# Cross-covariance attention: loads in 4 KB rows, softmax of eight heads at once, V transposed to two partition halves, stores in 2 KB rows

## The chip, the cores and the metric

The kernel runs on one core of one Trainium2 chip. The metric is the device time of one execution in microseconds (us). Before the change it was 144.62 us (median of 3 runs, 144.57 to 145.19). The profile's span, from first to last instruction, is shorter than the time: by 1.5 us in the profiled run of this kernel.

"Slow" is a run more than 1.5% above the fastest of the same kernel. Ratios are the mean time of one kernel's fast runs over the mean of the other kernel's fast runs of the same rounds on the same chip, with a 95% interval, so they are not quite the ratio of the medians quoted beside them. Where I turn a difference of two ratios into microseconds I multiply it by 144.7, the time of the kernel before, and say so.

## The reference

```python
# Q, K, V: (8, 12, 512, 64) float32, so 96 heads of 512 rows x 64
Q_norm = Q / (np.linalg.norm(Q, axis=-2, keepdims=True) + 1e-10)   # norm over the 512 rows
K_norm = K / (np.linalg.norm(K, axis=-2, keepdims=True) + 1e-10)
attn = np.einsum('bhnd,bhne->bhde', Q_norm, K_norm)                # 64 x 64 per head
attn = softmax(attn, axis=-1)
return np.einsum('bhnd,bhde->bhne', V, attn)
```

The logits are 64 x 64 per head, so the arithmetic is small and 50.33 MB have to move: 37.75 in and 12.58 out.

Both kernels get the squared norms and the raw logits from one product. With Q and K of a head side by side as `[Q | K]`, the gram matrix `[Q | K]^T [Q | K]` has the squared norms of Q and K on its diagonal and Q^T K off it.

## The kernel before

Four heads are a unit, and there are 24 units. Row `n` of a head lies on partition `n // 4`, so that one partition's share of one head is 4 rows x 64 floats, 1 KB.

```python
T, HU, PU = 4, 4, 2
Qf = Q.rearrange("b h (p t) d -> p (b h) t d", p=128)       # K, V, out alike: 1 KB runs

def casts(u):                                               # all on VectorE
    ... four casts of Q and K halves into qkb ...
    nc.vector.tensor_copy(w.rearrange("p t h d -> p h t d"), vf[u])
def grams(u):                                               # 16 matmuls of 128 rows per unit
    for h in range(HU):
        for t in range(T):
            x = qkb[u][:, h, t, :]
            nc.tensor.matmul(o, x, x, start=(t == 0), stop=(t == T - 1))
# norms (4 masked reductions), power -0.5 on GpSimd, scale_k, logits, exps,
# normalise: each per unit, in pieces of two heads            ... cut ...
def vtrans(u):                                              # 8 transposes, 2 copies per unit
def outs(u):                                                # 8 matmuls, 2 copies per unit
```

Of the kernel before, what the change touches and what calls it, by code (L numbers as in the profile page):

```python
# [8 lines left out]
F32 = mybir.dt.float32  # L9
BF16 = mybir.dt.bfloat16  # L10
AF = mybir.ActivationFunctionType
ALU = mybir.AluOpType

D = 64
T = 4
HU = 4
PU = HU // 2


@with_exitstack  # L20
def kernel(
# [6 lines left out]
):  # L28
    nc = tc.nc
    B, H, N, _ = Q.shape  # L30
    assert N == 128 * T and Q.shape[3] == D
    BH = B * H
    U = BH // HU


    Qf = Q.rearrange("b h (p t) d -> p (b h) t d", p=128)
    Kf = K.rearrange("b h (p t) d -> p (b h) t d", p=128)
    Vf = V.rearrange("b h (p t) d -> p (b h) t d", p=128)
    Of = out.rearrange("b h (p t) d -> p (b h) t d", p=128)

    ctx.enter_context(tc.manual_schedule())

    const = ctx.enter_context(tc.tile_pool(name="const", bufs=1))
    qp = ctx.enter_context(tc.tile_pool(name="qp", bufs=5))
    vp = ctx.enter_context(tc.tile_pool(name="vp", bufs=5))
    vbp = ctx.enter_context(tc.tile_pool(name="vbp", bufs=3))
    qkp = ctx.enter_context(tc.tile_pool(name="qkp", bufs=4))
    vtp = ctx.enter_context(tc.tile_pool(name="vtp", bufs=4))
    sop = ctx.enter_context(tc.tile_pool(name="sop", bufs=10))
    small = ctx.enter_context(tc.tile_pool(name="small", bufs=4))  # L50
    ps_g = ctx.enter_context(tc.tile_pool(name="ps_g", bufs=2, space=bass.MemoryType.PSUM))
    ps_v = ctx.enter_context(tc.tile_pool(name="ps_v", bufs=2, space=bass.MemoryType.PSUM))
    ps_l = ctx.enter_context(tc.tile_pool(name="ps_l", bufs=2, space=bass.MemoryType.PSUM))
    ps_o = ctx.enter_context(tc.tile_pool(name="ps_o", bufs=2, space=bass.MemoryType.PSUM))

    LOAD_AHEAD = 3
    CAST_AHEAD = 1
    STORE_LAG = 6

    qf, kf, vf, vb, qkb, gram, nsq, kqs, rq, lg, ex, ab, vt, so = ({} for _ in range(14))  # L60

    def load_qk(u):
        qf[u] = qp.tile([128, HU, T, D], F32, name="qf")
        kf[u] = qp.tile([128, HU, T, D], F32, name="kf")
        nc.sync.dma_start(out=qf[u], in_=Qf[:, u * HU:(u + 1) * HU])  # L65
        nc.sync.dma_start(out=kf[u], in_=Kf[:, u * HU:(u + 1) * HU])  # L66

    def load_v(u):
        vf[u] = vp.tile([128, HU, T, D], F32, name="vf")
        nc.sync.dma_start(out=vf[u], in_=Vf[:, u * HU:(u + 1) * HU])  # L70

    def store(u):
        nc.sync.dma_start(out=Of[:, u * HU:(u + 1) * HU], in_=so[u])

    def casts(u):

        t_ = qkb[u] = qkp.tile([128, HU, T, 2 * D], BF16, name="qkb")
        nc.vector.tensor_copy(t_[:, 0::2, :, 0:D], qf[u][:, 0::2])  # L78
        nc.vector.tensor_copy(t_[:, 1::2, :, D:2 * D], qf[u][:, 1::2])  # L79
        nc.vector.tensor_copy(t_[:, 0::2, :, D:2 * D], kf[u][:, 0::2])  # L80
        nc.vector.tensor_copy(t_[:, 1::2, :, 0:D], kf[u][:, 1::2])  # L81

        w = vb[u] = vbp.tile([128, T, HU, D], BF16, name="vb")
        nc.vector.tensor_copy(w.rearrange("p t h d -> p h t d"), vf[u])  # L84

    def grams(u):
        g = gram[u] = ps_g.tile([128, PU, 4, D], F32, name="gram")
        for h in range(HU):
            o = g[:, h // 2, 2 * (h % 2):2 * (h % 2) + 2, :]
            for t in range(T):  # L90
                x = qkb[u][:, h, t, :]
                nc.tensor.matmul(o, x, x, start=(t == 0), stop=(t == T - 1))  # L92

    def norms(u):

        n2 = nsq[u] = small.tile([128, 2, PU], F32, name="nsq")
        for p in range(PU):
            for c, (blk, m) in enumerate(((gram[u][:, p, 0::3, :], mask_q), (gram[u][:, p, 1:3, :], mask_k))):
                scr = small.tile([128, 2, D], F32, name="scr")
                nc.vector.tensor_tensor_reduce(  # L100
                    out=scr, in0=blk, in1=m, scale=1.0, scalar=1e-20,
                    op0=ALU.mult, op1=ALU.add, accum_out=n2[:, c, p:p + 1],
                )
        r = rq[u] = small.tile([128, 2, PU], F32, name="rq")
        nc.gpsimd.tensor_tensor(out=r, in0=n2, in1=mhalf, op=ALU.pow)  # L105

    def scale_k(u):

        kk = kqs[u] = small.tile([128, PU, 2, D], F32, name="kqs")
        for p in range(PU):  # L110
            nc.vector.scalar_tensor_tensor(  # L111
                out=kk[:, p], in0=gram[u][:, p, 0::3, :], scalar=rq[u][:, 1, p:p + 1], in1=off_diag,
                op0=ALU.mult, op1=ALU.mult,
            )

    def logits(u):
        l = lg[u] = ps_l.tile([128, PU, D], F32, name="lg")
        for p in range(PU):
            nc.tensor.matmul(l[:, p, :], kqs[u][:, p].rearrange("p a d -> p (a d)"), eye2)  # L119

    def exps(u):
        e = ex[u] = small.tile([128, PU, D], F32, name="ex")
        s = small.tile([128, PU], F32, name="esum")
        for p in range(PU):
            nc.scalar.activation(e[:, p, :], lg[u][:, p, :], AF.Exp, scale=rq[u][:, 0, p:p + 1], accum_out=s[:, p:p + 1])  # L125
        ex[u] = (e, s)

    def normalise(u):
        e, s = ex[u]
        ri = small.tile([128, PU], F32, name="rinv")  # L130
        nc.vector.reciprocal(ri, s)  # L131
        a = ab[u] = small.tile([128, PU, 2, D], BF16, name="ab")
        for p in range(PU):
            nc.vector.scalar_tensor_tensor(  # L134
                out=a[:, p], in0=e[:, p, None, :].to_broadcast([128, 2, D]), scalar=ri[:, p:p + 1], in1=on_diag,
                op0=ALU.mult, op1=ALU.mult,
            )

    def vtrans(u):
        for p in range(PU):  # L140
            ps = ps_v.tile([128, T, 128], BF16, name="vps")
            for t in range(T):
                nc.tensor.transpose(ps[:, t, :], vb[u][:, t, 2 * p:2 * p + 2, :].rearrange("p h d -> p (h d)"), identb)  # L143
            w = vtp.tile([128, T, 128], BF16, name=f"vt{p}")
            nc.scalar.copy(w, ps)  # L145
            vt[u, p] = w

    def outs(u):
        s = so[u] = sop.tile([128, HU, T, D], F32, name="so")
        for p in range(PU):  # L150
            po = ps_o.tile([128, T, 2, D], F32, name="po")
            for t in range(T):
                nc.tensor.matmul(po[:, t], vt[u, p][:, t, :], ab[u][:, p].rearrange("p a d -> p (a d)"))  # L153
            nc.scalar.copy(s[:, 2 * p:2 * p + 2].rearrange("p h t d -> p t h d"), po)  # L154


    for u in range(LOAD_AHEAD):
        load_qk(u)
        load_v(u)

    ident = const.tile([128, 128], F32, name="ident")
    make_identity(nc, ident)
    identb = const.tile([128, 128], BF16, name="identb")
    nc.gpsimd.tensor_copy(identb, ident)
    mask_q = ident.rearrange("p (a d) -> p a d", a=2)
    swap = const.tile([128, 2, D], F32, name="swap")
    nc.gpsimd.tensor_copy(swap[:, 0, :], ident[:, D:])
    nc.gpsimd.tensor_copy(swap[:, 1, :], ident[:, :D])
    mask_k = swap
    eye2 = const.tile([128, D], F32, name="eye2")  # L170
    nc.gpsimd.tensor_tensor(out=eye2, in0=ident[:, :D], in1=ident[:, D:], op=ALU.add)
    blocks = const.tile([128, 3, D], F32, name="blocks")
    nc.gpsimd.memset(blocks, 0.0)
    nc.gpsimd.memset(blocks[0:D, 1, :], 1.0)
    nc.gpsimd.memset(blocks[D:, 0, :], 1.0)
    nc.gpsimd.memset(blocks[D:, 2, :], 1.0)
    off_diag = blocks[:, 0:2, :]
    on_diag = blocks[:, 1:3, :]
    mhalf = const.tile([128, 2, PU], F32, name="mhalf")
    nc.gpsimd.memset(mhalf, -0.5)  # L180

    for u in range(CAST_AHEAD):
        casts(u)
    for s in range(U + 2):
        if s + LOAD_AHEAD < U:
            load_qk(s + LOAD_AHEAD)
            load_v(s + LOAD_AHEAD)
        if 0 <= s - STORE_LAG:
            store(s - STORE_LAG)
        if s < U:  # L190
            grams(s)
            norms(s)
        if 0 <= s - 1 < U:
            logits(s - 1)
            exps(s - 1)
        if s < U:
            vtrans(s)
        if s + CAST_AHEAD < U:
            casts(s + CAST_AHEAD)
        if 0 <= s - 1 < U:  # L200
            normalise(s - 1)
        if s < U:
            scale_k(s)
        if 0 <= s - 2 < U:
            outs(s - 2)
    for u in range(U + 2 - STORE_LAG, U):
        store(u)


# [28 lines left out]
```

## Time and profile before

| | before |
|---|---|
| time, median | 144.62 us |
| span | 143.1 us |
| DMA | full in all slices but the first and last, 50701 packets, nearly all of 1 KB, 353 GB/s |
| VectorE | 100.9 us busy (71%) |
| TensorE | 95.3 us busy (67%), 864 matmuls and 864 weight loads |
| ScalarE, GpSimd | 64.8 us (45%), 29.9 us (21%) |

Read the DMA row first: it is what never rests. The engines' busy shares say that none is full. The list of DMA queues: queue, kind, packets, MB, share of sixteen engines.

```profile
q8 instruction: 6, 0.10, 0.3%
```

By the kind that the page gives it, this queue brings instructions, not data.

### The profile page before, as it was taken

Reading aid. Unit: us, or ns where it says so; the run is one execution under the profiler, and the core shown is the slowest. Engines: PE = TensorE matmul, PEld = TensorE weight load, DVE = VectorE, ACT = ScalarE, POOL = GpSimd, SP = SyncE. Lnnn points to the kernel's source line nnn. Section 1 sums busy time; section 2 is a strip of 40 time slices with the busy share of each in tenths; the row PEclk is TensorE's granted clock in tenths of the full one; section 3 lists DMA queues with packets and bytes.
Section 4 is the critical chain, followed back from the end, with each engine's and each line's share of the span. In section 5 each row is a group of like instructions: output and inputs, shape, how many; then the busy total and the mean of one; then the engine's idle time right before and its main releaser. Section 6 shows DMA issues by size and latency. Waiting matters only on the chain.

```text
span 143.1 us, 2715 instructions
## 1 busy us (share of the span) xinstructions
PE 95.3 (67%) x864; PEld 83.7 (59%) x864; DVE 100.9 (71%) x432; ACT 64.8 (45%) x193; POOL 29.9 (21%) x39
## 2 busy tenths in 40 slices
PE   0245879775896797686559874776795694397820
PEld 0234669664795686575557763765694683397620
DVE  0435888989888987696786886883868868767410
ACT  3003406764377644715706536437074273371840
POOL 6003302332033330311302303302022032031100
PEclk9999999999559856857975589655559559855555
DMA  4999999999999999999999999999999999999993
GB/s 133 336 353 349 348 348 351 350 348 348 348 350 348 376 370 378 368 371 384 368 372 380 372 376 379 371 380 371 375 369 369 371 382 372 382 377 386 377 322 113
DMA packets 50701, 50.49 MB, mean 353 GB/s; under 512 B 1536, under 2 KB 50688, under 8 KB 50688
## 3 DMA queue, kind: packets, MB, share of 16 engines
q1 hardware_dynamic: 50688, 50.34, 104.5%
q8 instruction: 6, 0.10, 0.3%
q14 instruction: 7, 0.06, 0.1%
HBM read 37.75 MB, written 12.58 MB: 352 GB/s over the span
## 4 chain that ended last, share of the span: by engine, by line
DMA 65%; DVE 14%; SPq 12%; PE 2%; ACT 1%; issue 1%; ACTq 0%
DMA vf<-in_V_dram 59%; DMA qf<-in_Q_dram 6%; SPq L65 5%; DVE vb L84 4%; SPq L66 4%; DVE ab L134 4%; SPq L70 3%; DVE scr L100 3%; DVE kqs L111 2%; PE lg L119 2%; ACT ex L125 1%; DVE rinv L131 1%; PE po L153 0%; ACT so L154 0%; DVE qkb L78 0%
## 5 line engine op out<-in xcount | busy, mean ns | idle before, releaser
L92 PE MATMUL gram<-qkb 128*128 128x128 bf16 x384 | 39.6, 283 | 20.0 <-DVE qkb L80 19.4
L105 POOL TENSOR_TENSOR rq<-nsq,mhalf 128x4 f32<-128x4 f32 x24 | 27.6, 1151 | 102.0 <-DVE nsq L100 102.0
L92 PEld LDWEIGHTS <-qkb 128*128 128x128 bf16 x384 | 33.8, 130 | 25.3 <-DVE qkb L80 24.6
L125 ACT ACTIVATE ex<-lg,rq 128x64 f32<-128x64 f32 x48 | 14.7, 310 | 63.2 <-PE lg L119 63.2
L119 PE MATMUL lg<-eye,kqs 128*128 128x64 f32 x96 | 22.8, 381 | 19.4 <-DVE kqs L111 19.3
L119 PEld LDWEIGHTS lg<-eye,kqs 128*128 128x128 f32 x96 | 18.8, 271 | 24.9 <-DVE kqs L111 24.9
L145 ACT COPY vt<-vps 128x512 bf16<-128x512 bf16 x48 | 25.7, 593 | 8.7 <-PE vps L143 8.7
L84 DVE CAST vb<-vf 128x1024 bf16<-128x1024 f32 x24 | 16.7, 694 | 15.2 <-DMA vf<-in_V_dram 15.2
L154 ACT COPY so<-po 128x512 f32<-128x512 f32 x48 | 26.4, 618 | 0.3 <-PE po L153 0.3
L143 PE MATMUL vps<-identb,vb 128*128 128x128 bf16 x192 | 20.9, 274 | 1.9 <-DVE vb L84 1.9
L153 PE MATMUL po<-ab,vt 128*128 128x128 bf16 x192 | 20.9, 274 | 0.6 <-DVE ab L134 0.6
L143 PEld LDWEIGHTS <-vb 128*128 128x128 bf16 x192 | 19.3, 138 | 2.2 <-DVE vb L84 2.2
L80 DVE CAST qkb<-kf 128x512 bf16<-128x512 f32 x24 | 10.2, 424 | 11.6 <-DMA kf<-in_K_dram 11.6
L153 PEld LDWEIGHTS <-vt 128*128 128x128 bf16 x192 | 17.4, 129 | 0.9 <-DVE ab L134 0.9
L134 DVE SCALAR_TENSOR_TENSOR ab<-ex,rinv,blocks 128x128 bf16<-128x128 f32 x48 | 14.7, 349 | 0.9
L111 DVE SCALAR_TENSOR_TENSOR kqs<-gram,rq,blocks 128x128 f32<-128x128 f32 x48 | 14.5, 344 | 0.0
L78 DVE CAST qkb<-qf 128x512 bf16<-128x512 f32 x24 | 10.2, 425 | 5.1 <-DMA qf<-in_Q_dram 5.1
L100 DVE CUSTOM_DVE_ANT_0 scr<-gram,swap 128x128 f32<-128x128 f32 x48 | 13.7, 286 | 0.0
L100 DVE CUSTOM_DVE_ANT_0 scr<-gram,ident 128x128 f32<-128x128 f32 x48 | 13.6, 284 | 0.0
L79 DVE CAST qkb<-qf 128x512 bf16<-128x512 f32 x24 | 10.1, 420 | 0.0
L81 DVE CAST qkb<-kf 128x512 bf16<-128x512 f32 x24 | 10.1, 419 | 0.0
L125 ACT ACTIVATION_READ_ACCUMULATOR ex<-lg,rq 128x1 f32 x48 | 9.4, 196 | 0.0
(18 smaller groups left out, 15.8 us busy)
## 6 DMA issues: line engine op xcount, KB each, us to landing
qf<-in_Q_dram SPq DMA_DIRECT2D x24, 512.0 KB, 8.3
kf<-in_K_dram SPq DMA_DIRECT2D x24, 512.0 KB, 8.4
vf<-in_V_dram SPq DMA_DIRECT2D x24, 512.0 KB, 8.4
out_dram<-so SPq DMA_DIRECT2D x24, 512.0 KB, 7.9
```

The costliest lines, as they stand in the source:

```text
L84: nc.vector.tensor_copy(w.rearrange("p t h d -> p h t d"), vf[u])
L92: nc.tensor.matmul(o, x, x, start=(t == 0), stop=(t == T - 1))
L100: nc.vector.tensor_tensor_reduce(out=scr, in0=blk, in1=m, scale=1.0, scalar=1e-20, op0=ALU.mult, op1=ALU.add, accum_out=n2[:, c, p:p + 1],)
L105: nc.gpsimd.tensor_tensor(out=r, in0=n2, in1=mhalf, op=ALU.pow)
L111: nc.vector.scalar_tensor_tensor(out=kk[:, p], in0=gram[u][:, p, 0::3, :], scalar=rq[u][:, 1, p:p + 1], in1=off_diag, op0=ALU.mult, op1=AL ...
L119: nc.tensor.matmul(l[:, p, :], kqs[u][:, p].rearrange("p a d -> p (a d)"), eye2)
L125: nc.scalar.activation(e[:, p, :], lg[u][:, p, :], AF.Exp, scale=rq[u][:, 0, p:p + 1], accum_out=s[:, p:p + 1])
L134: nc.vector.scalar_tensor_tensor(out=a[:, p], in0=e[:, p, None, :].to_broadcast([128, 2, D]), scalar=ri[:, p:p + 1], in1=on_diag, op0=ALU. ...
L143: nc.tensor.transpose(ps[:, t, :], vb[u][:, t, 2 * p:2 * p + 2, :].rearrange("p h d -> p (h d)"), identb)
L145: nc.scalar.copy(w, ps)
L153: nc.tensor.matmul(po[:, t], vt[u, p][:, t, :], ab[u][:, p].rearrange("p a d -> p (a d)"))
L154: nc.scalar.copy(s[:, 2 * p:2 * p + 2].rearrange("p h t d -> p t h d"), po)
```

## The change

The intent is fewer and longer DMA rows. Partition `32 h + p` now holds sixteen consecutive rows of head `h`: 16 x 64 floats, 4 KB, and a load of four heads is one contiguous block of 512 KB. The price is that a head has only 32 partitions, so its gram product needs 16 matmuls of 32 rows instead of 4 of 128. VectorE is relieved by doing norms, scaling, softmax and products for two units (eight heads, the two partition halves) at once, and by giving the V cast to GpSimd.

```diff
-T = 4
+T = 16
-    Qf = Q.rearrange("b h (p t) d -> p (b h) t d", p=128)
+    Qu = Q.rearrange("b h (p t) d -> (b h p) (t d)", t=T)           # 4 KB rows
+    Of = ... .rearrange("(s r i p x) -> s i p r x", r=2, i=2, p=128, x=J * D)   # 2 KB rows
     def grams(u):
-        g = ps_g.tile([128, PU, 4, D], F32)                # 2 buffers
+        g = ps_g.tile([128, HU, 512], F32)                 # 512 floats per head, 1 buffer
-        for h in range(HU):
-            for t in range(T):
-                x = qkb[u][:, h, t, :]
+        for t in range(T):
+            for h in range(HU):
+                x = qkb[u][32 * h:32 * (h + 1), t, :]
+                nc.tensor.matmul(g[:, h, 0:2 * D], x, x, ...)
+    def cast_v(u):
+        nc.gpsimd.tensor_scalar(out=vb[u], in0=v32[u], scalar1=1.0, scalar2=0.0, ...)
+    def squares(u):   # per unit: two diagonal picks, one copy of the K^T Q block, into halves
+    def norms(s):     # per pair: one reduction, one power (GpSimd)
+    def scale_k(s):   # per pair: kqs = kq * r
     def vtrans(s, k):
+        for c in range(2):
+            for j in range(J // 2):
+                for r in range(2):      # unit r of the pair to partition half r
+                    nc.tensor.transpose(ps[r * D:(r + 1) * D, c, j, :], vb[2 * s + r][:, t, :], identb)
     ... logits, exps, normalise, outs per pair of units; one buffer each of ps_g, ps_v, ps_l ...
+    for s in range(U + 4):              # the order in which each engine gets its work
+        p, odd = divmod(s, 2)
+        ... loads and stores ...
+        cast_qk(s + 1)
+        cast_v(s - 1)
+        if not odd: scale_k(p - 1)
+        if odd:     normalise(p - 1)
+        grams(s); squares(s)
+        if odd:     norms(p)
+        if not odd: outs(p - 2, 3); logits(p - 1); exps(p - 1); vtrans(p - 1, 0)
+        if odd:     vtrans(p - 1, 1); outs(p - 1, 0); outs(p - 1, 1); outs(p - 1, 2)
```

(Bounds tests on the last lines left out.)

## The prediction

Its sum came to 130.3 us of span along the last V and 128.3 for the transfers, so to 131.0 us of time. Three quarters of the bytes at 414 and one quarter at 393, its estimates from the packet records, give 408.5. Its "row groups" are the four sets of 32 partitions, one for each head of a unit. That matmuls on them run at once, and that GpSimd and VectorE can block each other, were assumptions: the trace of before shows neither.

> **What bounds the kernel now.** I read the slices of the page first, because they show whether one limit holds from end to end or whether stages differ.
>
> ```profile
> PE   0245879775896797686559874776795694397820
> DVE  0435888989888987696786886883868868767410
> ACT  3003406764377644715706536437074273371840
> PEclk9999999999559856857975589655559559855555
> DMA  4999999999999999999999999999999999999993
> GB/s 133 336 353 349 348 348 351 350 348 348 348 350 348 376 370 378 368 371 384 368 372 380 372 376 379 371 380 371 375 369 369 371 382 372 382 377 386 377 322 113
> DMA packets 50701, 50.49 MB, mean 353 GB/s; under 512 B 1536, under 2 KB 50688, under 8 KB 50688
> ```
>
> The DMA row is 9 in all slices but the first and the last, and no engine's row is. The GB/s row is flat, and it has two levels: about 349 while only loads run (slices 2 to 12), about 375 once stores are mixed in. The packet line says in what sizes: 50688 packets under 2 KB, of which 1536 are the small ones that signal a landing. The other 49152 carry 50.33 MB, so each is 1024 bytes. That is one (head, partition) row: 4 x 64 floats.
>
> Next the queue and the chain, to see whether the transfers themselves are what is waited for.
>
> ```profile
> q1 hardware_dynamic: 50688, 50.34, 104.5%
> ...
> DMA 65%; DVE 14%; SPq 12%; PE 2%; ACT 1%; issue 1%; ACTq 0%
> DMA vf<-in_V_dram 59%; DMA qf<-in_Q_dram 6%; SPq L65 5%; DVE vb L84 4%; SPq L66 4%; DVE ab L134 4%; SPq L70 3%; DVE scr L100 3%; DVE kqs L111 2%; PE lg L119 2%; ACT ex L125 1%; DVE rinv L131 1%; PE po L153 0%; ACT so L154 0%; DVE qkb L78 0%
> ```
>
> The packets' time fills all sixteen engines for the whole span and a bit more (packets overlap). The chain runs through the landing of loads for 65% of the span, and another 12% is the queue's own issuing. VectorE's 14% of the chain is work between a landing and a buffer coming free, not work that starves the DMA. The waits confirm the direction: VectorE waits for data, and TensorE waits for VectorE.
>
> ```profile
> PE gram L92 <- DVE qkb L80: 19.4, 16, 6.3
> ...
> DVE vb L84 <- DMA vf<-in_V_dram: 15.2, 24, 2.8
> DVE qkb L80 <- DMA kf<-in_K_dram: 11.6, 17, 1.4
> ```
>
> Last, a view by stretches, for the end.
>
> ```profile
> 20.00:36.00 16.00, 12.28 (x132) 10.94 (x133) 14.74 (x68) 9.60 (x31) 5.03 (x4) 0.99 1.10 349
> ...
> 84.00:108.00 24.00, 16.74 (x144) 14.79 (x144) 17.27 (x74) 10.56 (x32) 4.34 (x4) 0.64 1.09 374
> ...
> 130.00:143.00 13.00, 5.83 (x40) 5.03 (x40) 3.63 (x19) 5.38 (x16) 1.01 (x1) 0.50 0.84 292
> ```
>
> The columns are busy time of PE, weight loads, DVE, ACT and POOL, then the granted clock, the DMA share and GB/s. Full sharing is about 1.09; only the last 13 us fall short (0.84). So the kernel is bound by the rate at which 1 KB packets move, plus some 3 us lost at the end.
>
> [...]
>
> **The change part by part.**
>
> *Loads.* The same 72 loads of 512 KB, in 4096-byte rows: 9216 packets instead of 36864. From the trace's packet records, a 1024-byte packet has a median of 46 ns, and the 8192-byte packets that fetch instructions take 307 to 309 ns at best. The line through both gives 37.4 ns per 1024 bytes ((308 - 46)/7) and 8.6 ns per packet. Then a 4096-byte packet takes about 158 ns, which on 16 engines is 414 GB/s (an estimate). [...]
>
> *Stores.* 24 of 512 KB in 2048-byte rows: 83.4 ns, 393 GB/s by the same estimate. [...]mixing gained 7% in before (375 against 349), which may or may not repeat. I take 408 over the whole stream.
>
> *VectorE.* Out: four casts of 128x512 at about 422 ns, a V cast at 694, four reductions at 285 plus four accumulator reads at 83, one reciprocal, four scalings at about 346: 1.69 + 0.69 + 1.47 + 0.16 + 1.38 = 5.4 us per unit by durations (4.2 by busy time, 100.9/24, because they overlap). In, per unit: two casts of 128x1024 at 694 = 1.39; two diagonal picks over 256 elements, an estimate of 344 + 128 x 1.05 = 480 ns each (twice the cast's slope of (694 - 424)/512) = 0.96; a copy of 256, about 0.4. Per pair of units: a reduction over 512 about 0.7, a scaling of 256 about 0.45, a reciprocal 0.16, two products of 256 about 0.9. Together 2.75 + 2.2/2 = 3.9 by durations, so about 3.3 busy.
>
> *GpSimd* takes the V cast. Its own set-up copies in before take 238 ns for 64 columns and 292 for 128 (a cast), so 0.84 ns per element: about 1.05 us for 1024, or 2 if the form is slower. With half a power of 1.2 to 2 us per unit it has 3 us at most.
>
> *ScalarE*: the exponentials stay 48; the V copies are 24 of twice the size, the output copies 48 as before. About 60 us in all, as now (64.8).
>
> *TensorE* gets the most new work. Matmuls per pair of units: grams 2 x 64 with 32 rows each (now 2 x 16 with 128), logits 16 records (8), transposes 32 (16), outputs 32 (16). Back to back, this trace has 107 ns per 128-column matmul at half clock (16 in 1.89 us: (1.89 - 0.31)/15) and 56 at full clock (8 in 0.61 us: (0.61 - 0.22)/7). If four row groups run at once, grams cost 14 to 27 ns each, and I allow 27: 3.5 us. Logits about 1 to 2, transposes and outputs 64 x 56 = 3.6 at full clock. With about 1.5 for the waits on the single transpose buffer and the two output buffers: about 9.6 us per pair.
>
> *The budget.* A pair moves 8 x 524288 bytes = 4.19 MB; at 408 GB/s that is 10.3 us. VectorE needs 6.6, ScalarE 5, GpSimd 6 at most, TensorE about 9.6. All lie beside the transfers.
>
> *The sum.* First packet at 1.9 us (as now). The last V load comes when about 2.3 MB of stores are left: 48.0/0.408 = 117.7, so at 119.6 us. After that: V cast 1.1, two rounds of transposes and copies through one buffer about 4.3, outputs about 2, last store about 3.3: 10.7 us (now 14.3, from 128.8 to 143.1). That makes 130.3. Filling the DMA alone and adding the 3 us now lost gives 1.9 + 123.4 + 3 = 128.3. Middle: 129.5 of span, plus the 1.5 us by which the time now exceeds the span: **131.0 us**.
>
> **The rivals.** *TensorE becomes the bound.* The gram of a unit has one set of buffers, so grams, picks and the next grams follow each other. If the row groups don't overlap, grams cost 56 ns each: 7.2 us per pair, in all 13 us, and 12 x 13 makes about 160. At half clock without overlap it is worse. For it: the clock in before is only 0.5 to 0.7 in the second half. Against: [...]the records at 26.74 us have a weight load, a matmul and the next weight load starting within 15 ns, so issuing alone doesn't cost 56. *The rate doesn't rise to 408*, because 375 may already be what the memory gives when loads and stores alternate: 1.9 + 50.33/0.385 + 3 + 1.5 = 137. Against: 16 engines x 1024/46 ns is almost exactly the 356 that packets back to back would give, so the cost is per packet. *GpSimd's casts and VectorE's casts block each other*: an added 1 us per unit on VectorE still fits (4.3 of 5.1), so the time would hardly move. *Mixing gains again*: 425 GB/s gives 1.9 + 118.4 + 3 + 1.5 = 125.
>
> **Range and chances.** The DMA cases span 125 to 137; TensorE as partial bound pulls up. I put 126 to 138 at 8 in 10. Faster by over 2% (below 141.7) 0.90: a fifth of the expected 13.6 us is enough. Within 2% 0.06, slower 0.04, both for TensorE as the bound.
>
> **What would show it.** Right: 9216 + 6144 + 1536 = about 16,900 packets, GB/s above 400 in the middle slices, the DMA row still at 9, casts waiting for landings, gram matmuls starting well under 56 ns apart. Wrong: DMA slices falling to 7 or 8 with TensorE or VectorE at 9; a GB/s row at 375 with full DMA (rate rival); power instructions or V casts on GpSimd of 2 us and more with VectorE casts stretched beside them (lock rival); or a last stage longer than 11 us after the last V load.

## The result, and the profile after

The changed kernel takes 140.56 us in the median of four runs (138.82 to 141.48), the kernel before 144.59 beside it. The ratio of fast runs is 0.9633 (0.9576 to 0.9689): faster by 3.7%. The predicted 131.0 us and its range of 126 to 138 were both missed.

Two of the four runs count as slow (141.48 and 141.13), and the profiled one is the first of them, with a span of 139.7 us. The fast ones have spans of 137.0 and 138.2. What makes the slow runs 2 us longer I did not find; their mean granted TensorE clocks, 0.82 and 0.89, against 0.83 and 0.84 of the fast ones, do not set them apart. I use this profile for where time goes, and the ratios for how much. The profiles of several variants below, taken in fast runs, show the same gaps.

The slices of the changed kernel:

```profile
PE   0225584795565954656966557946937745966440
DVE  2347786798798867848797977886795977543200
DMA  4999999999999999999999999999999999707016
GB/s 156 364 409 418 407 409 405 412 407 406 407 412 409 419 406 411 415 412 411 410 418 408 416 409 410 419 413 416 406 415 410 411 413 349 274 22 292 11 69 232
DMA packets 16920, 50.69 MB, mean 363 GB/s; under 512 B 1536, under 2 KB 1536, under 8 KB 16896
```

The transfers did what was predicted: 16,920 packets, 405 to 419 GB/s from the third slice on. But from slice 34 on the GB/s row falls, to 22 and 11 in two slices of the last five, where before kept above 320 up to the last. The same by stretches (busy time of PE, weight loads, DVE, ACT and POOL, then granted clock, DMA share and GB/s):

```profile
84.00:108.00 24.00, 16.66 (x500) 13.75 (x502) 18.54 (x34) 13.96 (x32) 11.11 (x8) 0.78 1.03 413
108.00:128.00 20.00, 13.14 (x374) 10.77 (x372) 13.63 (x27) 12.35 (x29) 7.85 (x7) 0.84 0.75 289
128.00:140.00 12.00, 4.53 (x71) 3.63 (x68) 1.02 (x3) 5.88 (x14) 0.00 (x0) 0.50 0.35 130
```

No engine is full in any of these stretches, and yet the DMA starves at the end. Something serial is late. The chain that ended last now hardly touches the DMA:

```profile
PE 40%; ACT 22%; issue 13%; DVE 10%; POOL 5%; DMA 5%; SPq 1%; POOLq 0%; ACTq 0%
```

The 13% of "issue" is time in which an engine waited for nothing that the profile shows. Which engine, the list of waits says (engine, line, what for: us in total, times, longest), next to VectorE's longest wait:

```profile
DVE kqs L114 <- POOL r L110: 12.6, 12, 1.8
PEld L89 <- issue: 10.8, 14, 2.3
PE gram L89 <- issue: 10.3, 8, 2.2
```

Before had 1% of "issue" in its chain. One such gap in time order (start, duration, engine, line, operation, count, and in brackets the idle time before it):

```profile
78.99 0.62 PE L89 MATMUL gram<-qkb 32*128 32x128 bf16 x31
81.77 0.66 PE L89 MATMUL gram<-qkb 32*128 32x128 bf16 x33 [2.16 <-issue]
```

The 64 grams of one unit stop dead after 31, for 2.16 us, and go on. Nothing in the program lies between the 31st and the 32nd. The queue of instructions shows what else changed:

```profile
q1 hardware_dynamic: 16896, 50.34, 90.8%
q8 instruction: 19, 0.31, 0.9%
```

Nineteen packets of 16,384 bytes where before had six. From the records I counted TensorE's instructions, matmuls and weight loads together. There are 4992 of them (1728 before). Gaps put down to "issue" begin after instructions 959, 1215, 1471, 1727, 1983, 2239, then 3007, 3263, 3519, 4031, 4287 and 4543. Neighbours are 256 apart or a multiple of 256. Together these twelve gaps are 14.7 us. Each ends 2.3 to 2.6 us after such a packet starts, and in a run of neighbours the packet starts 3.6 to 3.8 us after TensorE went on across the boundary before. I call 256 instructions a page from here on. In a row, TensorE resumes at 38.40, 44.60, 50.79, 56.99 and 63.19 us: one page each 6.2 us, whatever part of a pair's work lay in it.

The end of the kernel, in time order:

```profile
125.89 1.25 DVE L114 TENSOR_TENSOR kqs<-kq,r 128x256 f32<-128x256 f32 x1 [1.84 <-POOL r L110]
...
128.25 1.07 PE L148 MATMUL vps<-identb,vb 128*64 128x128 bf16 x16
...
129.60 1.30 ACT L152 COPY vt<-vps 128x1024 bf16<-128x1024 bf16 x1
...
133.40 1.08 PE L163 MATMUL po<-ab,vt 128*64 128x128 bf16 x16 [0.96 <-ACT vt L152]
...
135.40 0.58 ACT L164 COPY so<-po 128x512 f32<-128x512 f32 x1 [0.24 <-PE po L163]
```

The last load of K landed at 112.47 us and the last of V at 119.95. The logits of the last pair start at 127.20, after the first line, and the transposes of V, which come after the logits in TensorE's order, at 128.25. The last V cast too stands behind this pair's power on GpSimd, and ran at 125.83. That is 8.3 us after their data arrived. From the logits to the end of the span it is 12.5 us.

### The profile page after: what moved, and what is told of

It reads as the page before. It is cut to its first block, busy times and chain, and to the rows that moved or that the text cites. A ratio compares the mean times of both kernels' runs of the same rounds, so it can differ in the third digit from the quotient of the medians.

```text
span 139.7 us, 5665 instructions
## 1 busy us (share of the span) xinstructions
PE 84.4 (60%) x2496; PEld 69.6 (50%) x2496; DVE 95.4 (68%) x183; ACT 71.9 (51%) x169; POOL 50.0 (36%) x45
## 2 busy tenths in 40 slices
DMA packets 16920, 50.69 MB, mean 363 GB/s; under 512 B 1536, under 2 KB 1536, under 8 KB 16896
## 4 chain that ended last, share of the span: by engine, by line
PE 40%; ACT 22%; issue 13%; DVE 10%; POOL 5%; DMA 5%; SPq 1%; POOLq 0%; ACTq 0%
PE gram L89 15%; ACT vt L152 14%; PE po L163 9%; PE vps L148 8%; PE lg L121 7%; ACT ex L128 6%; POOL r L110 5%; DMA qk<-in_K_dram 5%; DVE kqs L114 3%; DVE scr L99 2%; DVE n L108 1%; DVE ab L137 1%; DVE kq L104 1%; ACT L128 1%; ACT so L164 1%
## 5 line engine op out<-in xcount | busy, mean ns | idle before, releaser
L89 PE MATMUL gram<-qkb 32*128 32x128 bf16 x1536 | 37.1, 259 | 21.3 <-issue 10.3
L110 POOL TENSOR_TENSOR r<-n,mhalf 128x8 f32<-128x8 f32 x12 | 23.2, 1932 | 57.6 <-DVE n L108 38.0
L89 PEld LDWEIGHTS <-qkb 32*128 32x128 bf16 x1536 | 30.2, 115 | 23.7 <-issue 10.8
L152 ACT COPY vt<-vps 128x1024 bf16<-128x1024 bf16 x24 | 31.2, 1301 | 16.4 <-PE vps L148 16.4
L77 DVE CAST qkb<-qk 128x1024 bf16<-128x1024 f32 x48 | 32.3, 712 | 6.6 <-DMA qk<-in_K_dram 3.8
L163 PE MATMUL po<-ab,vt 128*64 128x128 bf16 x384 | 23.7, 257 | 17.4 <-ACT vt L152 13.3
L81 POOL TENSOR_SCALAR vb<-v 128x1024 bf16<-128x1024 f32 x24 | 25.8, 1078 | 18.6 <-DMA v<-in_V_dram 17.4
L99 DVE SCALAR_TENSOR_TENSOR scr<-gram,eye 64x256 f32<-64x256 f32 x48 | 20.2, 421 | 7.8 <-PE gram L89 7.3
L148 PE MATMUL vps<-identb,vb 128*64 128x128 bf16 x384 | 18.8, 251 | 8.7 <-ACT vt L152 7.7
L114 DVE TENSOR_TENSOR kqs<-kq,r 128x256 f32<-128x256 f32 x12 | 14.2, 1186 | 12.6 <-POOL r L110 12.6
L148 PEld LDWEIGHTS <-vb 128*64 128x64 bf16 x384 | 14.9, 128 | 12.3 <-issue 10.3
L121 PE MATMUL lg<-eye,kqs 64*64 64x64 f32 x96 | 11.0, 276 | 3.5 <-DVE kqs L114 3.5
L122 PE MATMUL lg<-eye,kqs 64*64 64x64 f32 x96 | 11.0, 276 | 0.0
L137 DVE TENSOR_TENSOR ab<-ex,rinv 64x256 bf16<-64x256 f32 x24 | 10.3, 429 | 0.6
(12 smaller groups left out, 12.8 us busy)
## 6 DMA issues: line engine op xcount, KB each, us to landing
qk<-in_Q_dram SPq DMA_DIRECT2D x24, 512.0 KB, 10.1
qk<-in_K_dram SPq DMA_DIRECT2D x24, 512.0 KB, 10.1
```

The source lines that it names most:

```text
L77: nc.vector.tensor_copy(t_[:, :, x * D:(x + 1) * D], qk32[u][:, x])
L81: nc.gpsimd.tensor_scalar(out=t_, in0=v32[u], scalar1=1.0, scalar2=0.0, op0=ALU.mult, op1=ALU.add)
L89: nc.tensor.matmul(g[:, h, 0:2 * D], x, x, start=(t == 0), stop=(t == T - 1))
L99: nc.vector.scalar_tensor_tensor(out=scr[s][half, HU * (x ^ r):HU * (x ^ r) + HU], in0=g[half, :, half], scalar=1e-20, in1=eye2[half, None ...
L110: nc.gpsimd.tensor_tensor(out=t_, in0=n2, in1=mhalf, op=ALU.pow)
L121: nc.tensor.matmul(l[LO, h, :], kqs[s][HI, h, :], eye2[HI])
```

## The experiments

Two readings stood at the start. The expectations call them FETCH and BUFFER. FETCH: TensorE's instruction stream has three times as many instructions, its pages arrive too slowly, and the kernel is limited by the number of TensorE instructions. BUFFER: the single buffers of PSUM tiles, that of the V transposes above all, hold TensorE up. Later rounds put three more beside them: Q and K come too late, GpSimd's V cast blocks VectorE, and VectorE's program order forms a loop.

To compare kernels I use three marks of each profile: when the logits of the first pair start, when those of the twelfth and last pair start, and the span. The difference of the first two over 11 is the pace, and what follows the second is the drain.

| run | result correct | time, median us | ratio of fast runs to before (95%) | first logits | last pair's logits | pace | drain |
|---|---|---|---|---|---|---|---|
| after (slow profile) | yes | 140.56 | 0.9633 (0.9576 to 0.9689) | 18.13 | 127.20 | 9.92 | 12.5 |
| wide | no | 137.62 | 0.9504 (0.9478 to 0.9531) | 18.92 | 123.72 | 9.53 | 12.1 |
| merged | yes | 137.25 | 0.9488 (0.9453 to 0.9522) | 19.17 | 123.58 | 9.49 | 12.0 |
| early2 | yes | 140.77 | 0.9769 (0.9692 to 0.9847) | 18.45 | 125.48 | 9.73 | 12.4 |
| resident | no | 131.41, one run | | 17.44 | 116.77 | 9.03 | 12.8 |
| castlast | yes | 141.64 | 0.9782 (0.9707 to 0.9856) | 17.70 | 126.90 | 9.93 | 12.5 |
| merged_castlast | yes | 137.72 | 0.9502 (0.9445 to 0.9559) | 17.80 | 123.45 | 9.60 | 12.5 |
| merged_castlast_nolock | no | 134.99 | 0.9290 (0.9214 to 0.9367) | 18.32 | 119.70 | 9.22 | 12.5 |
| merged_castlast_vsplit | yes | 136.28 | 0.9411 (0.9365 to 0.9457) | 17.84 | 121.63 | 9.44 | 12.5 |

"No" marks kernels that compute something else.

### First round: the instruction stream and the buffers

**wide**: grams with 256 moving columns, two steps of `t` in one matmul: half the gram matmuls, as many columns streamed, a wrong result. 3456 TensorE instructions instead of 4992.

```diff
-        for t in range(T):
+        for t in range(0, T, 2):
-                nc.tensor.matmul(g[:, h, 0:2 * D], x, x, ...)
+                y = qkb[u][32 * h:32 * (h + 1), t:t + 2, :].rearrange("p t d -> p (t d)")
+                nc.tensor.matmul(g[:, h, 0:4 * D], x, y, ...)
```

> Half as many gram matmuls, each with twice the moving columns (wrong result on purpose); TensorE instructions fall from 4992 to 3456, its column work stays. Theory FETCH (TensorE is fed one 16 KB page of 256 instructions per about 6.1 us while the DMA engines are full, 416 instructions per pair = 9.9 us): no more bound by pages, last V load still near 119 us, compute caught up, time 130 to 133. Theory BUFFER (single transpose buffer and in-order ScalarE copies set 9.9 us per pair): 138 to 141, as the changed kernel. Theory LOCK (GpSimd's V cast blocks VectorE's scaling in the chain): 138 to 141.

137.62 us. The gaps are gone entirely (0 us of "issue" on page boundaries, against 14.7), so FETCH was right about what they are. But the time fell by 3 us in the medians and by 1.3% in the ratios, about 1.9 us of the 144.7. It did not come near 130 to 133. The gaps were real, and most of their time went to other waiting.

**tiny**: one more matmul of one column after every second step, into a corner of PSUM that nobody reads. 32 more matmuls per unit, 6528 TensorE instructions, almost no arithmetic. The result stays right.

```diff
                 nc.tensor.matmul(g[:, h, 0:2 * D], x, x, ...)
+                if t % 2 == 0:
+                    nc.tensor.matmul(g[:, h, 256:257], x, x[:, 0:1], start=False, stop=False)
```

> 32 one-column matmuls more per unit into an unused column (right result): 128 TensorE instructions more per pair, 6528 in all. FETCH: 128/256 of 6.1 us = 3.05 us more per pair, 36 us in all, time 170 to 178, and the gaps still 256 instructions apart. Only their own TensorE time (at most 29 ns each, 1.9 us per pair, if all of it were on the path): at most 162. BUFFER and LOCK: under 150.

162.67 us in its one run, 22 us more than after. Sixteen gaps on page boundaries sum to 22.9 us, and the longest is:

```profile
75.98 0.21 PE L89 MATMUL gram<-qkb 32*128 32x128 bf16 x1 [3.00 <-issue]
```

The time lies under the 170 to 178 of FETCH, so FETCH missed in size. It lies above what the other readings allow, but by only 0.7 us of one run where the added matmuls' own TensorE time was allowed 162. What speaks for the pages here is the gaps, not the total. Between instructions 1215 and 4543, from 33.98 to 111.79 us, the thirteen pages come 6.0 us apart: there the stream of pages is the bound. After the loads have ended they come 3.5 to 4.3 us apart, and this softens the end. In after a pair has 416 instructions, and 416/256 x 6.2 = 10.1 us: the pages alone would pace it at about what it has, 9.92. So wide's small gain suggests that something else has nearly the same pace.

**psv2**: two buffers for the V transposes, paid for by letting the logits share the outputs' buffers.

```diff
-    ps_v = ... bufs=1     ps_l = ... bufs=1
+    ps_v = ... bufs=2     # no ps_l; logits in the rotation of ps_o
```

> Two PSUM buffers for the transposes; the logits take a turn in the output buffers' rotation. BUFFER: the second transposes no longer wait for the first copy, about 0.8 us less per pair, 130 to 133. FETCH: pages still set the pace, 138 to 141. LOCK: 138 to 141.

142.2 us, ratio 0.9802 (0.9765 to 0.9839): a little slower than after. Its profile, of a fast run, has 18.5 us of "issue" gaps. BUFFER is refuted as the main cause, though with the reserve that the logits now waited for the outputs' buffers.

**merged**: the same relief of TensorE as wide, with a right result. The casts of V for both units go into one tile, and one 128-column transpose does what two of 64 columns did. 4608 TensorE instructions.

```diff
-        t_ = vb[u] = vbp.tile([128, T, D], BF16)
+        vb[s] = vbp.tile([128, T, 2, D], BF16)      # one per pair; unit r casts into [:, :, r, :]
-                for r in range(2):
-                    nc.tensor.transpose(ps[r * D:(r + 1) * D, c, j, :], vb[2 * s + r][:, t, :], identb)
+                nc.tensor.transpose(ps[:, c, j, :], vb[s][:, t].rearrange("p r d -> p (r d)"), identb)
```

> V of the two units cast side by side, so one 128-column transpose replaces two of 64 columns (right result): 32 TensorE instructions fewer per pair, 4608 in all. FETCH: 384/256 of 6.1 us = 9.15 us per pair, below the 10.2 us of the transfers, 130 to 134. BUFFER: the transposes' own time falls by about 0.45 us per pair, 134 to 138. LOCK: 137 to 141.

137.25 us, and 0.4 us of page gaps. It is correct and faster than after, by 1.45% of 144.7, 2.1 us. Its slices and chain changed kind:

```profile
DMA  4999999999999999999999999999999999968026
DMA 81%; ACT 6%; PE 4%; DVE 2%; issue 2%; POOL 1%; SPq 1%; ACTq 0%
```

The chain goes through the loads again, and the drain remains. So after this round the question was what delays the last pair when TensorE is no longer starved of instructions.

### Second round: load order, the floor of the transfers, the V cast

**early** and **merged_early**: Q and K loaded six units ahead instead of four, V lagging by four instead of two, on top of after and of merged. The thought: if the chain hangs on the landing of K, bring K earlier.

```diff
-    LA = 4       VLAG = 2      qp bufs=5
+    LA = 6       VLAG = 4      qp bufs=7
```

> The changed kernel with Q and K loaded six units ahead instead of four (seven buffers instead of five), V as before, so the last K should land about two V loads and two stores earlier (5 us of transfers; 112.5 in the changed kernel). FETCH and TAIL together (pages pace the loop, then the last pair's serial chain runs after the last K): the loop is still paged, so casts wait less and gain little, 137 to 141. TAIL alone (only the landing of the last K counts): 133 to 137. TRANSFERS (the end is set by the queued stores): as the changed kernel, 139 to 141.

> Merged transposes and the early Q and K in one kernel. FETCH and TAIL: without the page stalls, the last K's chain (22.9 us from landing to end with merged transposes alone) starts up to 5 us earlier, until the last V's own chain of about 11 us after 119 binds: 131 to 135. TRANSFERS: as merged alone, 137.

143.72 us (ratio 0.9913) and 141.0 us (0.9717): both slower than what they were built on. The last K landed at 108.07 us in early, 4.4 us sooner, but the logits of the first pair started at 22.82 us, 4.7 us later, and those of the last at 130.08. The list of waits of merged_early says why:

```profile
POOL vb L83 <- DMA v<-in_V_dram: 52.0, 15, 16.3
```

In GpSimd's program a V cast stands ahead of the power, so the later V made the softmax wait for V: VectorE's scaling waited for the power up to 4.3 us at a time, against 1.8 in merged. (In early itself GpSimd's wait is 35.2 us, and the longest of the scaling 5.6.)

**dma_only**: the transfers of after with no computing, stores from a constant tile.

```diff
-    cast_qk(0) ... the whole computing loop
+    # loads and stores in the same order only
```

> All loads and stores in the same order, stores from one constant tile, no other work (wrong result on purpose). What the transfers alone need: 1.9 + 50.33/0.410 + about 2 = 126.7 of span, 127 to 130 of time, by every theory; if it is above 134, TRANSFERS explains the miss.

128.02 us, span 126.2, the DMA row at 9 up to the last slice. This is the floor of the transfers. The prediction's 128.3 us of span for the transfers plus loss was close to it.

**nolock**: the V cast cut to a sixteenth, the rest of the V tile constant, so that GpSimd has little left to do beside VectorE but the power.

```diff
-        nc.gpsimd.tensor_scalar(out=t_, in0=v32[u], ...)
+        nc.gpsimd.tensor_scalar(out=t_[:, 0:1], in0=v32[u][:, 0:1], ...)
```

> GpSimd casts only a sixteenth of V (wrong result on purpose), so it no longer blocks VectorE's scaling of K (1186 ns on average, 420 in the one case without a cast beside it). LOCK: 0.75 us less per pair, 9 us in all, 130 to 133. FETCH and TAIL: the loop stays at the pages' pace and only the drain's own scaling and cast are saved, 138 to 140.5.

139.09 us, ratio 0.962: the same as after. But the scaling, VectorE's product of `kq` and `r`, fell from 1186 ns to 458 ns in the mean. In after's own trace the eleven scalings that start some 0.06 us after a V cast took 1253 to 1257 ns each, and the one that started just ahead of its cast, at 17.65 us, took 425: that is the "one case" of the expectation. The block is real. In nolock's own profile, of a fast run, the page gaps are 15.2 us, and from 30.68 to 115.03 us the instruction packets start 5.9 to 6.3 us apart: the pages, I read, took up what it freed.

### Third round: is it the order, and is it memory at all

**early2**: merged and early together, with the power moved ahead of the V cast on GpSimd. **early2_drain**: the same with half of the last pair's copies on VectorE. **merged_powfirst**: merged with the power ahead of the cast, without the earlier loads.

```diff
-        cast_v(s - 1)                # before scale_k
         ...
         if odd: norms(p)
+        cast_v(s - 1)
# early2_drain, last pair only: second V copy and two output copies
-        nc.scalar.copy(...)
+        nc.vector.tensor_copy(...)
```

> Merged transposes, Q and K six units ahead, and on GpSimd the power is issued before the V cast (before, the power stood behind a cast that waited for its V: GpSimd waited 52 us for V in the early kernel). TAIL: the last pair's logits and exponentials are done before the last V lands at about 119, and only V's own chain is left: cast 1.1, two transposes and copies through one buffer about 4.6, outputs about 2.6, store about 3.8: 131 of span, 131 to 134 of time. TRANSFERS or another cause of the drain: as the merged kernel, 136 to 138.

> The same, and for the last pair alone VectorE takes the second V copy and two of the four output copies from ScalarE. TAIL: about 1 us less than early2. Otherwise no change.

> Merged transposes and the power ahead of the V cast, loads as in the changed kernel. TAIL: the last K still lands near 112.7 and its chain is unchanged but for the V cast, which overlaps the scaling as before: 136 to 138, as merged. If the order on GpSimd alone were the cause, 131 to 134.

140.77 us (0.9769), 140.33 us (0.9701) and 137.9 us (0.9528). All three missed an improvement on merged. In early2 the last K landed at 107.47, and the logits of the last pair still came only at 125.48. Loading earlier cannot help a loop that does not keep up. It also brought a wait of its own, which merged has for 0.4 us only, and which may be why early2 is slower than merged: TensorE, in its program order, stands before the transposes until V is cast.

```profile
PEld L149 <- POOL vb L83: 12.9, 9, 4.5
```

**resident**: loads only for the first four units, later units reuse those tiles; stores kept, all computing kept, wrong result. No load is ever waited for after the first 20 us or so.

```diff
     def load_qk(u):
+        if u >= 4:
+            qk32[u] = qk32[u % 4]
+            return
     # load_v alike
```

> The changed kernel with loads for the first four units only, whose data is used over and over (wrong result on purpose); stores stay. FETCH: with the DMA engines a quarter busy the pages come sooner (3.5 to 4.5 us apart at most, as after the loads' end in the changed kernel), the gaps 256 instructions apart shrink or vanish, and a pair takes clearly less than 9.9 us: 120 to 130 in all. If the pages took their 6.1 us whatever the DMA does: 137 to 141. BUFFER: the pair still takes 9.9 us, 137 to 141, without gaps at pages.

131.41 us, in one run. This is the most telling run: with a DMA that mostly idles, with no page gap on TensorE, the kernel still takes longer than the transfers alone. Its DMA row, its chain, and one turn of the loop in time order:

```profile
DMA  4999940044080350530802513504408008126034
DVE 39%; ACT 16%; POOL 16%; PE 14%; DMA 5%; issue 4%; SPq 1%; POOLq 0%; ACTq 0%
...
60.08 1.92 POOL L116 TENSOR_TENSOR r<-n,mhalf 128x8 f32<-128x8 f32 x1 [4.73 <-DVE n L114]
62.03 1.26 DVE L120 TENSOR_TENSOR kqs<-kq,r 128x256 f32<-128x256 f32 x1 [0.92 <-POOL r L116]
64.13 0.31 ACT L134 ACTIVATE ex<-lg,r 128x64 f32<-128x64 f32 x1 [1.46 <-PE lg L128]
65.84 0.85 DVE L143 TENSOR_TENSOR ab<-ex,rinv 64x256 bf16<-64x256 f32 x2
66.73 0.86 DVE L105 SCALAR_TENSOR_TENSOR scr<-gram,eye 64x256 f32<-64x256 f32 x2
68.06 0.69 DVE L114 TENSOR_REDUCE n<-scr 128x8 f32<-128x512 f32 x1
68.92 1.92 POOL L116 TENSOR_TENSOR r<-n,mhalf 128x8 f32<-128x8 f32 x1 [4.74 <-DVE n L114]
```

Read the start times downward. The power of this pair starts at 60.08. Scaling, logits, exponentials, products follow, each waiting for the one above. The products end at 66.69, and only then may VectorE take the picks of the next pair's odd unit, because they stand behind the products in its program. Then the copy, the reduction, and the next pair's power, at 68.92. One turn is 8.84 us, and the pace over the whole run is 9.03. No engine is full in it. It is a ring that goes once through GpSimd, VectorE, TensorE and ScalarE for every pair. The blocked scaling is still in it, with 1185 ns in the mean.

### Fourth round: changing the ring

**castlast**, **merged_castlast**: VectorE casts the next Q and K after the reduction, not first in the step. **merged_castlast_drain**: with the shared copies for the last pair.

```diff
-        cast_qk(s + 1)               # first in the step
         ...
         if odd: norms(p)
+        cast_qk(s + 1)
```

> The same order in the changed kernel, with its 4992 TensorE instructions. ORDER and FETCH: pages of 6.1 us still set 9.9 us per pair, so casts don't wait for landings and the order changes little: 138 to 141. ORDER alone: 135 to 137.5.

> Merged transposes, and VectorE issues the cast of the next unit's Q and K last in each step, behind the previous pair's scaling and the picks (right result). ORDER: from the last K's landing (112.7) only cast 1.3, grams 1.1 to 1.9, picks 1.3, reduction 0.7, power 1.65, scaling 1.3 remain before the last logits, about 120.5 instead of 123.6: 3 us less, 133 to 135.5. DRAIN: no change, 136.5 to 138.

> merged_castlast, and for the last pair VectorE takes the second V copy and two of four output copies. 0.5 to 1.5 us less than merged_castlast if these copies lie on the last chain: 132 to 134.5.

141.64 us (0.9782), 137.72 us (0.9502) and 138.47 us (three of six runs slow; the fast ones 136.8 to 137.3, ratio 0.9461, 0.9384 to 0.9538). Moving the casts did not shorten the ring: merged_castlast paces 9.60 and merged 9.49. But it took the load waits off it. The shared copies of merged_castlast_drain brought no clear gain: its interval and that of merged_castlast overlap. The chain of merged_castlast is a pure view of the ring:

```profile
DVE 46%; PE 20%; POOL 14%; ACT 10%; issue 4%; DMA 3%; SPq 0%; POOLq 0%; ACTq 0%; DVEq 0%
```

castlast has only 2.9 us of page gaps, and still its pace is 9.93, as slow as after's. The packet records suggest why. From 29.75 to 115.37 us its instruction packets start 5.9 to 6.5 us apart (mean 6.12), as evenly as in after (6.0 to 6.6, mean 6.17), and 416/256 x 6.12 = 9.9. The mean follows from the pace by arithmetic; what speaks is the evenness, for in wide the packets lie 6.6 to 10.6 apart and in merged_castlast 5.8 to 7.2. So pages may pace castlast too, with most of their time hidden behind waits that the list puts to semaphores, and the sum of the gaps is no full measure of what the pages cost. No run tests this.

**merged_castlast_nolock**, **merged_nolock**: with the V cast cut to a sixteenth. **merged_castlast_vsplit**: the whole V cast, a correct kernel, but in four pieces of 256 elements, so that each should block VectorE for a shorter time.

```diff
# vsplit
-        nc.gpsimd.tensor_scalar(out=vb[s][:, :, r, :], in0=v32[u], ...)
+        for c in range(0, T, 4):
+            nc.gpsimd.tensor_scalar(out=vb[s][:, c:c + 4, r, :], in0=v32[u][:, c:c + 4], ...)
```

> merged_castlast with GpSimd casting only a sixteenth of V (wrong result on purpose). LOOP: scaling falls from 1117 to about 440 ns and the products by about 0.25 us per pair, so about 1 us less per pair: the loop falls to 8.0 to 8.6 us, the casts wait for landings again, the last logits start near 120.5 and the time is 133 to 135.5. If the loop isn't what holds the last pair back: 137 to 138.5, as merged_castlast.

> merged with the same small V cast. LOOP: the casts already wait for landings there (16.6 us), so the gain is mostly in the drain, 0.8 to 1.5 us: 135.5 to 137.

> merged_castlast with each V cast in four pieces (right result), so that VectorE is blocked for one piece of about 0.4 us at a time. LOOP: about half the gain of merged_castlast_nolock, 135 to 137.

134.99 us (0.9290), 135.95 us (0.9382) and 136.28 us (0.9411). Against their bases the ratios fall by 2.1%, 1.1% and 0.9%: 3.1, 1.5 and 1.3 us of 144.7. (The intervals of vsplit and of merged_castlast overlap slightly, so the last is likely rather than certain.) The scaling of after and then of merged_castlast_nolock, in the list of groups (line, engine, operation, shapes, count, busy us, mean ns, idle before it):

```profile
L114 DVE TENSOR_TENSOR kqs<-kq,r 128x256 f32<-128x256 f32 x12 | 14.2, 1186 | 12.6 <-POOL r L110 12.6
```

```profile
L116 DVE TENSOR_TENSOR kqs<-kq,r 128x256 f32<-128x256 f32 x12 | 5.3, 440 | 14.2 <-POOL r L112 14.2
```

With most of the page gaps out of the way the block shows a price, since the scaling lies in the ring. The scaling is 0.7 us shorter, and the pace falls by 0.38, from 9.60 to 9.22. The expectation had put it at 8.0 to 8.6, so something else binds before that. The packet records point at the pages again: from 30.57 to 109.70 us they start 5.8 to 6.3 us apart (mean 6.09), 384/256 x 6.09 = 9.1, and 3.2 us of page gaps are back. vsplit answers a rival, that nolock gains because GpSimd has less to do: there GpSimd's casts take 47.8 us instead of 26.1, and the scaling still falls, to 520 ns. merged_castlast_vsplit is the best correct kernel, with 5.9% off the kernel before, where after has 3.7%.

## Why the prediction was wrong

**What held.** The rate: predicted 408 GB/s, measured 405 to 419 in the full slices. Packets of 4096 bytes take 159 ns in the median (predicted 158), those of 2048 bytes 84 ns (predicted 83.4). The last V load landed at 119.95 us (predicted 119.6). The row groups overlap: in the 64 grams at 70.28 us the first four, one per head, start within 10 ns, and all 64 take 1.07 us at a granted clock of 1.00, (1.07 - 0.22)/63 = 13.5 ns apart, so the rival "TensorE becomes the bound by 56 ns per matmul" is out (the 64 grams at 26.22 us, at 0.50, take 1.89 us, some 25 ns apart by the same sum with 0.31, still within the 27 allowed). The V cast at 1078 ns (predicted 1.05 us) and the power at 1932 ns (1.2 to 2) were sized well. So were its lengths for VectorE, estimates, most without a source, but for the scaling: the picks took 421 ns (predicted 480), the copy 419 (0.4 us), the reduction 686 (0.7), the two products 429 each (0.9 together). VectorE's busy time was 95.4 us, where 3.3 a unit makes 79: the blocked scalings are 9 us of that.

**The step that failed** is the sentence in the budget: "All lie beside the transfers." It set the busy time of each engine per pair against 10.3 us and found each smaller. That test says that no engine is full. It doesn't say that a pair can pass in 10.3 us through all of them in turn, when the engines take their work in program order (GpSimd stood 52.0 us before V casts in merged_early, with the powers behind them) and one pair's products stand ahead of the next pair's picks. The ring costs 9.03 us a pair with no memory and no page gap in the way (resident), 9.92 in after. By its own figures the test was close, too: TensorE's "about 9.6" takes the logits at their lower end of 1 us, and with 2 it is 10.6, over 10.3.

Why 9.92 is too slow although it is under 10.3 is a second part of the same error. 10.3 us counts all the bytes of a pair, stores too. Early pairs have no stores yet, so loads come faster than that: 6 x 524288 bytes at 408 GB/s are 7.7 us (an estimate). The prediction's sum along the last V was 130.3 us of span (its middle of this and 128.3, given as 129.5, is 129.3), which with the measured drain of 12.5 needs the last pair's logits at 117.8. From the first logits at 18.13 that leaves (117.8 - 18.13)/11 = 9.06 us a pair. resident just does that. After doesn't: it comes 11 x (9.92 - 9.06) = 9.5 us late. That this adds up to the span of 139.7 is no check, since pace and drain were taken from the same profile; it only says where the time is. And that profile is of a slow run: the fast spans, 137.0 and 138.2, with the same fill and drain would mean a pace of 9.7 to 9.8 (an estimate).

**The term that moved** in the sum is the last: 10.7 us "after that", counted from the last V load. It measured 139.7 - 119.95 = 19.7 us. Its parts were not bad: transposes and copies 5.1 us (128.25 to 133.35; predicted 4.3), outputs 2.6 (predicted 2; the budget reckons both at full clock, and from 128 us on 0.50 was granted), last store 2.9 (issued at 136.01, landed at 138.86; predicted 3.3). But it began at 128.25, not at 119.95 plus a cast. TensorE's order puts the last pair's logits before the transposes, GpSimd's order puts its power before the last V cast, and both waited for the ring. The prediction's own warning, "a last stage longer than 11 us after the last V load", is what was seen.

**What made the ring slower than 9.06.** Two things are shown to be there and to cost time, and their shares overlap.

The first is TensorE's instruction pages, which the prediction did not think of. In after the packets have 16,384 bytes and the gaps lie 256 instructions apart. A pair has 4992/12 = 416 instructions. At 6.2 us a page, while the DMA is full, that is the 10.1 us worked out above, more than the ring's 9.03; merged has 384, 9.3 us. wide and merged remove the gaps and gain 1.9 and 2.1 us by the ratios. Both also shorten TensorE's work somewhat, and in merged 12 of 13 packets from 31.32 to 111.22 us still come within 6.2 us of the one before, so merged is not clear of the pages. wide is (6.6 us at least), and its pace is 9.53. In resident the DMA has room (0 to 8 tenths busy from the sixth slice on), pages come in time, and not one gap on a boundary is seen.

The second is the block between GpSimd and VectorE. The prediction named it as a rival and dismissed it: "an added 1 us per unit on VectorE still fits". The rival was tested against VectorE's busy time again. It was put for VectorE's casts. Of the 48 in after, 43 had next to no V cast beside them (43 ns at most) and took 688 ns in the mean; the five that ran into one took 720 to 1190. What is hit in every pair but the first is the scaling: 1253 to 1257 ns behind a V cast, 1186 in the mean of all twelve, 440 to 458 with that cast cut to a sixteenth. Why a V cast stretches it no run here shows. Since it lies in the ring, it counts once less else does: 3.1 us in merged_castlast, of the 8.1 us by which its twelve scalings got shorter, 1.5 in merged, nothing measurable in after (0.9633 against 0.962), where the pages seem to have filled the room.

**The rest.** With the block removed and the page gaps down to 3.2 us, 134.99 us (fast profile: span 132.2) remain, 4 us over the prediction. There the last K lands at 111.97, the last pair's logits follow 7.7 us later, and the drain is 12.5. The durations alone need about 6.1 us from that landing to the logits: one cast 0.7, grams 1.07, picks and copy 1.28, reduction 0.69, power 1.92, scaling 0.42 (an estimate from the rows above). So the true end of the chain hangs on K, not on V: some 6 + 12.5 us after 112, about 130.5 of span. The prediction came to nearly that figure by counting from V, with a path that was never the longest: that is luck.

**What stays open.** How the page gaps and the ring share the 2 us between after and merged; whether the pages pace castlast and merged_castlast_nolock, as the even packets suggest; why early2 is slower than merged; what the slow runs of after are. Not tried: the small V cast on top of wide, which would show the ring without block and without pages; and putting the odd unit's picks and the reduction ahead of the previous pair's products in VectorE's order, which by the loop shown for resident would take the exponentials and the products out of the ring.

## What to carry to other kernels

Busy time per engine against the transfer time is not a budget: also add up one turn of the serial ring that the engines' program orders form, and check that fill + turns x ring + drain ends when the transfers do, counted from each of the last loads. When a layout for the DMA is paid for in many small matmuls, count TensorE's instructions as well as their columns: pages of 256 took 6.2 us each beside a full DMA here. An instruction that another engine can block (here the scaling, 1254 ns behind a V cast instead of 425) matters by its place in the ring and not by its share of busy time.

## Figures measured in this case

- A page of 256 TensorE instructions came every 6.2 us while the DMA was full (after), and every 3.5 to 4.3 us in tiny after the loads had ended. In after, counting packets against boundaries, each page but the very last was fetched only when the one before it was being worked on.
- Loads in 4 KB rows and stores in 2 KB rows, mixed, moved at 405 to 419 GB/s in after. The records show 84 ns per packet of 2048 bytes and 159 per 4096 (after), and 46 per 1024 (before).
- ScalarE's copy of 1024 columns of 2-byte elements into the interleaved V, at a stride of two, took 1301 ns in after, where the contiguous copy of 512 in the kernel before took 593. No contiguous copy of 1024 was measured here, so what the stride alone costs stays open.
